# Hymba decoder layer: where the weight's tiles of the input projection begin in SBUF

## The chip, the cores and the metric

The kernel runs on one core of a Trainium2 chip. The metric is the device time of one execution, in microseconds. It is measured over three runs of the kernel before: median 2932.36 us, lowest 2932.19 us, highest 2941.21 us.

## The reference

One layer of a hybrid decoder over 2048 tokens of width 1024, all float32:

```python
h = RMSNorm(x);  z = h @ W_in + b_in        # 1024 -> 3600 columns, in groups of heads
y = concat[ FoX attention | mLSTM | HGRN2 ] # three causal mixers, each fed by its columns of z
x = x + y @ W_out
x = x + W_down( silu(conv3(h W_up)_gate) * conv3(h W_up)_up ),   h = RMSNorm(x)
```

The result must keep float32 accuracy, so each matmul operand is split into a high part (rounded to the type fp32r) and the low remainder. One product then takes three matmuls: high·high, high·low and low·high.

## The kernel before

The time divides into four stages: the input projection with the mLSTM and HGRN2 mixers woven into it (0 to about 940 us), the FoX attention (to about 1420 us), the output projection (to about 1650 us) and the feed-forward part (to the end).

**The input projection.** The 2048 tokens go in two halves, each in two blocks of 512 tokens. For a block, `z_norm` normalises x, transposes it and leaves `hhi` and `hlo`, each `[128, 8, 512]`: eight slices of the 1024 input features on the partitions, 512 tokens along the row. `z_groups` goes through 14 groups of 256 (two of them 264) output columns. `load_split` (L178) loads a group's weight into `wraw`, in two transfers of four feature slices each; ScalarE copies it to `whi` (L188) and GpSimd subtracts to get `wlo` (L189). Both are `[128, 8, width]` and have two buffers, so that the next group's weight is prepared while one is in use.

All the matmuls of the stage's projection are issued by the helper `mm3` (L193 to L198), eight feature slices by three products. There are two kinds of group:

- *Channel groups* (`ct_group`, L256; four of the 14). The weight is the stationary operand, 128 columns at a time, and the input streams past it: 512 tokens per matmul. 768 matmuls in all.
- *Token groups* (`nat_group`, L269; ten of the 14). The input is stationary, 128 tokens at a time, and the weight streams: 256 columns per matmul (3072 matmuls), or 264 in the two groups that carry gate columns as well (768 matmuls).

Every matmul is preceded by a load of its own 128 stationary columns (LDWEIGHTS, the rows PEld); the load for the next matmul runs while the present one streams. A stationary slice of 128 float32 is 512 bytes of a partition's row.

Between the projection's matmuls come the mixers' (`phase_b`, `phase_c`), which `merge` weaves in, and the order of the instructions on each engine is worked out by a planner that simulates the program with a cost model. So a tile that waits for another buffer can move instructions in this stage. Attention and the second feed-forward product have an order written out by hand.

**The other users of the same pattern.** `phase_out` (L1071) calls the same `mm3` at L198 for the output projection, with `yh`/`yl` stationary and `wohi`/`wolo` streaming, 512 columns. `product` in `ffn_up` (L1252) and `mm` in `ffn_down` (L1409) are the same three products, 512 columns each.

**Small tiles.** `z_stats` (L214) collects the second half's sums of squares in a tile `n8s` of its own. `padz` (L1589) is 96 bytes that nothing reads or writes. In `consts` (L1709) the function `cast` (L1713) loads nine constant masks through one scratch tile `craw` of 512 bytes and casts them; the first is used by `phase_c` at L728. The tag `z` has three buffers, through which every group's results leave (L263, L284).

**Where the tiles lie.** A partition's row is one range of bytes, and the pools hand it out in order; the remainders of the first bytes modulo 512, as the kernel before has them:

```
hhi, hlo (both blocks)            64
whi, wlo, first buffer           192      8448 bytes each = 16.5 x 512,
whi, wlo, second buffer          448      so the two buffers differ by 256
yh, yl, wohi, wolo               448      (output projection)
all operands at L1252 and L1409  448      (feed-forward)
```

A row of `whi` for one feature slice is 256 x 4 = 1024 bytes, or 1056 in the two wider groups, in which each slice begins 32 bytes further on.

Of the kernel before, what the change touches and what calls it, by code (L numbers as in the profile page):

```python
# [10 lines left out]
F32 = mybir.dt.float32  # L11
F32R = mybir.dt.float32r
# [9 lines left out]
P = 128  # L22
T = 2048
D = 1024
DT = D // P
# [81 lines left out]
def rms_scale(k, pool, out, ss, n, epsf, tag):  # L107

    for _ in rms_steps(k, pool, out, ss, n, epsf, tag):
        pass  # L110
# [67 lines left out]
def load_split(k, wp, src, tag="w", n=2):  # L178

    nc = k.nc  # L180
    width = src.shape[1]
    hi = k.t(wp, [P, DT, width], F32R, tag=tag + "hi")
    lo = k.t(wp, [P, DT, width], F32R, tag=tag + "lo")
    for q in range(0, DT, n):
        raw = k.t(wp, [P, n, width], tag=tag + "raw")
        nc.sync.dma_start(raw, src[q * P : (q + n) * P, :].rearrange("(dt p) c -> p dt c", p=P))
        h = hi[:, q : q + n, :]
        nc.scalar.activation(h, raw, AF.Copy)  # L188
        nc.gpsimd.tensor_tensor(lo[:, q : q + n, :], raw, h.bitcast(F32), op=ALU.subtract)  # L189
    return hi, lo  # L190
# [23 lines left out]
def z_stats(k, pz, xbufs):  # L214

    nc = k.nc
    ss = k.t(pz, [P, 8], tag="n8s", bufs=1)
    for b in range(2):
        for t in range(4):
            (x,) = z_load(k, 1, b, xbufs, t, 1)  # L220
            i = 4 * b + t
            nc.scalar.activation(x, x, AF.Square, accum_out=ss[:, i : i + 1])
    rstd = k.t(pz, [P, 8], tag="n8r", bufs=1)
    rms_scale(k, pz, rstd, ss, D, 1.0, "h")
    return rstd
# [1301 lines left out]
def _trunk(ctx, tc, a, out):  # L1527
    nc = tc.nc
    k = K(ctx, tc, a, out)

    def pool(stack, name, bufs, **kw):
        if kw.get("space") is not DRAM:
            kw["reuse_waits"] = "tile"
        return stack.enter_context(tc.tile_pool(name=name, bufs=bufs, **kw))
# [30 lines left out]
    with ExitStack() as ms:  # L1565
        cm = pool(ms, "cmix", 1)

        def mconst(name, shape, dt=F32, src=None):
            t = cm.tile(list(shape), dt, tag=name, name=name)
            if src is not None:  # L1570
                nc.sync.dma_start(t, src)
            return t

        bc = ExitStack()
        pb = pool(bc, "bc", 1, side="right")
        psb = pool(bc, "psb", 3, space=PSUM, side="right")
        k.q2 = pb.tile([P, 4, 2, P], F32, tag="q2", name="q2")
        nc.gpsimd.memset(k.q2, 0.0)
        with ExitStack() as zs:
            pz = pool(zs, "z", 2)  # L1580
            wp = pool(zs, "w", 2)
            psw = pool(zs, "psw", 3, space=PSUM)
            k.gmix = pz.tile([P, D], F32, tag="gmix", name="gmix", bufs=1)
            xb, xw = ((pb, "v", 2), (pb, "p4", 2)), ((pz, "x", 2),)
            k.hts = {}
            for _ in z_norm(k, 0, 0, pz, psw, xb):
                pass
            z = z_groups(k, 0, pz, wp, psw, xb)
            pz.tile([P, 24], F32, tag="padz", name="padz", bufs=1)  # L1589
            state(k, mconst)  # L1590
            for _ in range(ZC):
                next(z)
            consts(k, a, cp, mconst, pz, psw, cm)
            mix = mixers(k, pb, psb)
            merge(z, mix, RZ, XAT)
            late = late_consts(k, a, pz, psw)
            next(late)
            rstd = z_stats(k, pz, xw)
            merge(z, mix, RZ, 8)
            next(late)  # L1600
            xs = z_load(k, 1, 0, xw, 0, 2)
            merge(z, mix, RZ, 4)

            norm = z_norm(k, 1, 0, pz, psw, xw, xs, rstd)
            for _ in range(4):
                next(norm)
                merge(z, mix, RZ, 1)
            for _ in norm:
                pass
            for _ in z:  # L1610
                raise AssertionError("steps")
            merge(z_groups(k, 1, pz, wp, psw, xw, rstd), mix, RZ)
            for _ in mix:
                pass
        bc.close()
        wo = ExitStack()
        wor = ExitStack()
        with ExitStack() as at:

            k.pat = {n: pool(at, "at_" + n, 1) for n in ("ga", "oT", "B0", "B1", "A0", "A1", "V1", "o1")}  # L1620
            pa = pool(at, "att", 2)

            k.pat.update((n, pool(at, "at_" + n, 1)) for n in ("o0", "V0"))

            psa = {"m": pool(at, "psm", 3, space=PSUM, side="right")}
            psa.update((n, pool(at, "ps" + n, b, space=PSUM)) for n, b in (("s", 2), ("pv", 2), ("x", 1)))
            k.ga = k.pat["ga"].tile([P, 512], F32, tag="ga", name="ga", bufs=1)
            nc.sync.dma_start(k.ga, a["out_g"][0:1, 0:512].broadcast_to([P, 512]))
            side = {}
            w = w_out_load(  # L1630
                k, pool(wo, "wo", 1, side="right"), pool(wor, "wor", 1, side="right"), side, WO, WOS
            )
            attention(k, pa, psa, side)
# [75 lines left out]
def consts(k, a, cp, mconst, pz, psum, cm):  # L1709

    nc = k.nc

    def cast(dst, src):  # L1713
        raw = cm.tile([P, P], F32, tag="craw", name=k.nm("craw"))[:, 0 : src.shape[1]]
        nc.sync.dma_start(raw, src)
        nc.vector.tensor_copy(dst, raw)

    k.identb = mconst("identb", [P, P], BF16)
    k.mnat = mconst("mnat", [P, P], BF16)
    k.mtr = mconst("mtr", [P, P], BF16)  # L1720
    k.allneg = mconst("allneg", [P, P], BF16)
    k.cmask = mconst("cmask", [P, 7, HD], U8)
    nc.vector.tensor_copy(k.identb, k.ident)
    cast(k.mnat, a["mnat"])
    cast(k.mtr, a["mtr"])
    nc.vector.memset(k.allneg, NEG)
    for i in range(7):
        cast(k.cmask[:, i, :], a["cmask"][:, i * HD : (i + 1) * HD])

    k.sel8 = mconst("sel8", [72, BH])  # L1730
    nc.sync.dma_start(k.sel8[64:72], a["sel8"])
    k.bd = mconst("bd", [16, BH, P], F32R)
    sc = k.t(pz, [8, BH, P], tag="z", bufs=3)
    nc.vector.tensor_copy(sc, k.sel8[64:72].unsqueeze(2).broadcast_to([8, BH, P]))
    nc.sync.dma_start(k.bd[8:16].bitcast(F32), sc)
    k.sel2 = mconst("sel2", [BH, 2, P], F32, a["sel2"])
    k.gbc = mconst("gbc", [P, 512], F32, a["out_g"][0:1, 512:1024].broadcast_to([P, 512]))
    nc.vector.tensor_scalar(out=k.gbc, in0=k.gbc, scalar1=0.5, scalar2=None, op0=ALU.mult)

    b_in = a["b_in"][0]  # L1740
    pk = k.t(pz, [28, P], tag="pg")

    def row(r, src):
        nc.sync.dma_start(pk[r : r + src.shape[0] // P, :], src.rearrange("(c p) -> c p", p=P))

    row(0, b_in[OFF_BQK : OFF_BQK + 512])
    row(4, b_in[OFF_CQ : OFF_CQ + 512])
    for j in range(4):
        row(8 + 4 * j, a["b_conv_w"][0, j])
    row(24, a["lb_logits"][0])  # L1750
    for r, g in ((26, a["a_q_g"]), (27, a["a_k_g"])):
        for i in range(2):
            nc.sync.dma_start(pk[r : r + 1, i * HD : (i + 1) * HD], g)
    k.col = mconst("col", [P, 28])
    ps = k.t(psum, [P, 28], tag="t", bufs=2)
    nc.tensor.transpose(ps, pk, k.ident[0:28, 0:28])
    nc.vector.tensor_copy(k.col, ps)
    k.bcw = k.col[:, 8:24].rearrange("p (j c) -> p j c", c=4)
    k.gq, k.gk = k.col[:, 26:27], k.col[:, 27:28]
    nc.vector.tensor_scalar(out=k.gq, in0=k.gq, scalar1=HD**-0.5, scalar2=None, op0=ALU.mult)  # L1760

    lg = k.col[:, 24:26]
    lm, lr, lb = mconst("lm", [P, 2]), mconst("lr", [P, 2]), mconst("lb", [P, 2])
    nc.vector.tensor_tensor(lm, lg, lg, op=ALU.subtract)
    nc.scalar.activation(lm, lm, AF.Exp)
    nc.vector.reciprocal(lr, lm)  # L1766
    nc.vector.tensor_tensor(lr, lr, lm, op=ALU.mult)
    nc.vector.tensor_tensor(lb, lr, lr, op=ALU.subtract)
    nc.vector.tensor_scalar(out=lb, in0=lb, scalar1=0.0, scalar2=None, op0=ALU.max)
    k.lba, k.lbb, k.lbn = mconst("lba", [P, 2]), mconst("lbb", [P, 2]), mconst("lbn", [P, 2])  # L1770
    nc.vector.tensor_scalar(out=k.lbb, in0=lb, scalar1=-0.5, scalar2=0.5, op0=ALU.mult, op1=ALU.add)
    nc.vector.tensor_scalar(out=k.lbn, in0=k.lbb, scalar1=-1.0, scalar2=None, op0=ALU.mult)
    nc.vector.tensor_tensor(k.lba, lb, k.lbb, op=ALU.add)
# [45 lines left out]
```

## Time and profile before

| | |
|---|---|
| median of three runs | 2932.36 us |
| the profiled execution | 2937.63 us, its span 2935.5 us |
| TensorE (PE) busy | 2817.4 us, 96% of the span |
| weight loads (PEld) busy | 2342.7 us, 80% |
| VectorE (DVE), ScalarE (ACT), GpSimd (POOL) busy | 68%, 44%, 49% |
| mean granted TensorE clock | 0.977 of full speed |

PE is one row of matmuls, and PEld is the weight loads that run beside them. Matmuls are pipelined, and the records of consecutive ones overlap (a duration of 0.39 us, a start every 0.23 us); what a matmul costs is the distance from its start to the next one's start, which this document calls its pitch.

### The profile page before, as it was taken

To read this page: it belongs to the slowest core of one execution; us is meant where nothing else is said; L and a number is where in the kernel's file an instruction comes from. 1 tells how busy PE (TensorE), PEld (TensorE's weight loads), DVE (VectorE), ACT (ScalarE), POOL (GpSimd) and SP (SyncE) were. 2 spreads that over 40 slices of the span, in tenths; PEclk is the share of its full clock that TensorE was granted. 3 is DMA by queue.
4 is the path that set the end of the run, shared out by engine and by line. 5 is a ranking of instruction groups with operands and counts; after the bars stand their busy time and mean duration, and the time that the engine had idled before them with its cause. 6 is when DMAs were issued, how large, how long until landed. Compare 5 with 4: busy or idle time off the path is not lost. (4 is left out here: it accounts for less than half of the span.)

```text
span 2935.5 us, 42833 instructions
## 1 busy us (share of the span) xinstructions
PE 2817.4 (96%) x15181; PEld 2342.7 (80%) x15181; DVE 2005.9 (68%) x3384; ACT 1280.0 (44%) x2167; POOL 1435.1 (49%) x1199
## 2 busy tenths in 40 slices
PE   7999988999988999999899899999999999999999
PEld 7898987889988666666688788888788888888887
DVE  7337687265786787778546577677797577777655
ACT  4213323132322778878424344444454343444443
POOL 2245452334454577766302366666475644444443
PEclk9999997999999999999999999999999999999999
DMA  4424434333334554342257444444777333333666
GB/s 159 127 93 133 150 96 143 94 108 97 111 107 143 107 114 88 81 92 49 72 179 246 148 155 151 154 148 158 268 247 271 114 108 108 108 105 117 232 214 209
DMA packets 346615, 411.07 MB, mean 140 GB/s; under 512 B 47650, under 2 KB 234096, under 8 KB 343232
## 3 DMA queue, kind: packets, MB, share of 16 engines
q1 hardware_dynamic: 292016, 318.45, 37.2%
q10 hardware_dynamic: 51952, 81.45, 7.6%
q0 software_dynamic: 2432, 8.42, 0.8%
q8 instruction: 120, 1.97, 0.3%
q14 instruction: 95, 0.78, 0.1%
HBM read 280.24 MB, written 127.98 MB: 139 GB/s over the span
## 5 line engine op out<-in xcount | busy, mean ns | idle before, releaser
L1221 POOL TENSOR_TENSOR w<-w,w 128x512 fp32r<-128x512 f32 x302 | 404.8, 1353 | 403.3 <-ACT w L1220 339.2
L1409 PE MATMUL ps<-w,w 128*128 128x512 f32 x1848 | 420.9, 389 | 4.0 <-ACT w L1400 2.0
L1409 PEld LDWEIGHTS ps<-w,w 128*128 128x128 f32 x1848 | 346.6, 188 | 77.6 <-ACT w L1400 2.4
L198 PE MATMUL w<-whi,hhi 128*128 128x256 f32 (+1 forms) x1280 | 370.4, 289 | 3.1 <-DVE lr L1766 2.0
L198 PE MATMUL w<-whi,hlo 128*128 128x256 f32 (+1 forms) x1280 | 371.3, 290 | 0.0
L198 PE MATMUL w<-wlo,hhi 128*128 128x256 f32 (+1 forms) x1280 | 370.4, 290 | 0.6 <-POOL wlo L189 0.6
L898 POOL TENSOR_TENSOR pl<-pf,ph 128x512 fp32r<-128x512 f32 (+2 forms) x240 | 287.8, 1212 | 146.6 <-ACT ph L894 133.3
L1402 POOL TENSOR_TENSOR w<-w,w 128x512 fp32r<-128x512 f32 x154 | 216.3, 1412 | 200.9 <-ACT w L1400 155.4
L1220 ACT ACTIVATE w<-w 128x512 fp32r<-128x512 f32 x302 | 180.4, 627 | 258.7 <-POOL w L1221 86.7
L850 DVE TENSOR_REDUCE mx<-m 128x1 f32<-128x512 f32 (+2 forms) x320 | 190.8, 605 | 91.3 <-PE m L845 63.1
L1401 DVE TENSOR_TENSOR w<-w,w 128x512 fp32r<-128x512 f32 x154 | 179.9, 1178 | 103.4 <-ACT w L1399 102.0
L198 PEld LDWEIGHTS w<-whi,hhi 128*128 128x128 f32 x1280 | 245.2, 192 | 4.8 <-issue 3.8
L198 PEld LDWEIGHTS w<-wlo,hhi 128*128 128x128 f32 x1280 | 244.9, 191 | 2.7 <-POOL wlo L189 1.0
L198 PEld LDWEIGHTS w<-whi,hlo 128*128 128x128 f32 x1280 | 244.7, 191 | 1.8 <-issue 0.5
L892 ACT ACTIVATE pf<-s 128x512 f32<-128x512 f32 (+1 forms) x320 | 172.5, 539 | 91.1 <-PE s L886 50.9
L1226 DVE TENSOR_TENSOR w<-w,w 128x512 f32<-128x512 f32 x176 | 149.8, 870 | 85.3 <-DMA w<-in_w_up_dram 81.0
L189 POOL TENSOR_TENSOR wlo<-wraw,whi 128x1024 fp32r<-128x1024 f32 (+1 forms) x56 | 135.3, 2433 | 111.7 <-ACT whi L188 102.2
L894 ACT ACTIVATE ph<-pf 128x512 fp32r<-128x512 f32 (+1 forms) x320 | 185.1, 578 | 10.3
L1267 DVE SCALAR_TENSOR_TENSOR u<-ps,fcol,u 128x1023 f32<-128x1023 f32 x88 | 108.9, 1279 | 95.3 <-ACT u L1266 95.3
L913 PE MATMUL pv<-pl,V 128*65 128x512 f32 (+1 forms) x320 | 121.7, 380 | 25.2 <-DVE pl L898 24.3
L1400 ACT ACTIVATE w<-w 128x512 fp32r<-128x512 f32 x154 | 96.6, 628 | 111.3 <-PE ps L1409 88.7
L1399 ACT ACTIVATE w<-w 128x512 fp32r<-128x512 f32 x154 | 95.9, 623 | 89.8 <-POOL w L1402 44.4
(374 smaller groups left out, 7092.1 us busy)
## 6 DMA issues: line engine op xcount, KB each, us to landing
w<-in_w_up_dram SPq DMA_DIRECT2D x182, 256.0 KB
w<-s_g SPq DMA_DIRECT2D x154, 256.0 KB
w<-in_w_down_dram SPq DMA_DIRECT2D x110, 256.0 KB
wraw<-in_w_in_dram SPq DMA_DIRECT2D x48, 512.0 KB
s_g<-u ACTq DMA_DIRECT2D x88, 256.0 KB
w<-s_w SPq DMA_DIRECT2D x88, 256.0 KB
s_g<-w ACTq DMA_DIRECT2D x66, 256.0 KB
x<-in_x_dram SPq DMA_DIRECT2D x32, 512.0 KB
```

The costliest lines, as they stand in the source:

```text
L189: nc.gpsimd.tensor_tensor(lo[:, q : q + n, :], raw, h.bitcast(F32), op=ALU.subtract)
L198: nc.tensor.matmul(out, lsl(lhs[a], i), rsl(rhs[b], i), start=(i == 0 and j == 0), stop=(i == n - 1 and j == 2))
L850: nc.vector.tensor_reduce(mx[:, i, kb : kb + 1], m[:, 0:n], axis=AX.X, op=ALU.max)
L892: nc.scalar.activation(pf[:, c0:], s[:, c0:], AF.Exp)
L894: nc.scalar.activation(ph[:, c0:], pf[:, c0:], AF.Copy)
L898: eng.tensor_tensor(pl[:, c0:], pf[:, c0:], ph[:, c0:].bitcast(F32), op=ALU.subtract)
L1220: nc.scalar.activation(h, t, AF.Copy)
L1221: nc.gpsimd.tensor_tensor(lo, t, h.bitcast(F32), op=ALU.subtract)
L1226: nc.vector.tensor_tensor(t, x, y, op=op)
L1401: nc.vector.tensor_tensor(gl, gr, gh.bitcast(F32), op=ALU.subtract)
L1402: nc.gpsimd.tensor_tensor(wl, wr, wh.bitcast(F32), op=ALU.subtract)
L1409: nc.tensor.matmul(tiles[tile], g[x][:, tile * P : (tile + 1) * P], w[y], start=j == 0 and c == 0, stop=j == nj - 1 and c == 2,)
```

## The change

The two weight tiles get a fixed size of 17 x 128 float32 (8704 bytes, 17 x 512), of which the group uses the first 8 x width. To make room, and to move the pool's start, three small things go: `n8s` is taken from the existing tag `ss` (two buffers, otherwise used by the query and key groups), `padz` is removed, and `cast` takes its scratch from the tag `z` in place of `craw`.

```diff
@@ load_split
-    hi = k.t(wp, [P, DT, width], F32R, tag=tag + "hi")
-    lo = k.t(wp, [P, DT, width], F32R, tag=tag + "lo")
+
+    hi, lo = (
+        k.t(wp, [P, 17 * P], F32R, tag=tag + x)[:, 0 : DT * width].rearrange("p (n c) -> p n c", c=width)
+        for x in ("hi", "lo")
+    )
@@ z_stats
-    ss = k.t(pz, [P, 8], tag="n8s", bufs=1)
+    ss = k.t(pz, [P, 16], tag="ss")[:, 0:8]
@@ _trunk
             z = z_groups(k, 0, pz, wp, psw, xb)
-            pz.tile([P, 24], F32, tag="padz", name="padz", bufs=1)
             state(k, mconst)
@@ consts, cast
-        raw = cm.tile([P, P], F32, tag="craw", name=k.nm("craw"))[:, 0 : src.shape[1]]
+        raw = k.t(pz, [P, P], tag="z", bufs=3)[:, 0 : src.shape[1]]
         nc.sync.dma_start(raw, src)
         nc.vector.tensor_copy(dst, raw)
```

## Rows read from the trace of the kernel before

**Rows 1.** The page's head: span, busy time, PE in 40 slices and its clock.

```profile
span 2935.5 us, 42833 instructions
PE 2817.4 (96%) x15181; PEld 2342.7 (80%) x15181; DVE 2005.9 (68%) x3384; ACT 1280.0 (44%) x2167; POOL 1435.1 (49%) x1199
PEclk9999997999999999999999999999999999999999
```

**Rows 2.** Busy time by stretch: length, then busy us (instructions) of each engine, clock.

```profile
core 0: us, PE busy (x) PEld busy (x) DVE busy (x) ACT busy (x) POOL busy (x), PEclk, DMA share, GB/s
0.00:480.00 480.00, 440.54 (x3098) 407.82 (x3098) 302.64 (x657) 152.68 (x247) 186.29 (x187) 0.97 0.41 128
480.00:940.00 460.00, 441.31 (x3155) 405.71 (x3154) 294.47 (x646) 125.98 (x200) 188.34 (x180) 0.98 0.34 106
```

**Rows 3.** What TensorE waited for from 13 to 940 us: total, times, longest.

```profile
PE t L395 <- POOL z L391: 7.6, 6, 2.8
PE b L546 <- DVE cstate L763: 3.7, 1, 3.7
PE w L198 <- DVE lr L1766: 2.0, 1, 2.0
...
PE w L198 <- DVE cmask L1716: 1.1, 1, 1.1
```

**Rows 4.** Groups of matmuls by line and form: output<-inputs, count, busy and mean duration.

```profile
L198 PE MATMUL w<-whi,hlo 128*128 128x256 f32 x1024 | 297.9, 291 | 0.0
...
L198 PE MATMUL w<-hhi,wlo 128*128 128x512 f32 x256 | 101.7, 397 | 0.0
...
L198 PE MATMUL w<-whi,hlo 128*128 128x264 f32 x256 | 73.7, 288 | 0.0
```

**Rows 5.** Timeline, a channel group: start, duration, tile; 33 like them lie between.

```profile
111.10 0.39 PE L198 MATMUL w<-hlo,whi 128*128 128x512 f32 x1
...
119.03 0.39 PE L198 MATMUL w<-hhi,wlo 128*128 128x512 f32 x1
```

**Rows 6.** Timeline, output projection: 7 like them between the first two, 23 after.

```profile
1503.50 1.04 PE L1086 MATMUL ty<-ident,yin 128*128 128x128 f32 x8
...
1504.61 0.40 PE L198 MATMUL w<-wolo,yh 128*128 128x512 f32 x1
...
1506.46 0.39 PE L198 MATMUL w<-wohi,yh 128*128 128x512 f32 x1
...
1511.90 0.39 PE L198 MATMUL w<-wohi,yh 128*128 128x512 f32 x1
```

**Rows 7.** Timeline, second feed-forward product, 19 matmuls merged into one row.

```profile
2099.79 4.47 PE L1409 MATMUL ps<-w,w 128*128 128x512 f32 x19
```

**Rows 8.** Timeline, a token group of 256 columns; 94 like them lie between.

```profile
554.72 0.28 PE L198 MATMUL w<-whi,hhi 128*128 128x256 f32 x1
...
565.99 0.28 PE L198 MATMUL w<-whi,hlo 128*128 128x256 f32 x1
```

**Rows 9.** Timeline, a token group of 264 columns (38 between), and the mixer's matmuls after.

```profile
736.20 0.28 PE L198 MATMUL w<-whi,hlo 128*128 128x264 f32 x1
...
740.93 0.28 PE L198 MATMUL w<-whi,hlo 128*128 128x264 f32 x1
741.06 1.05 PE L721 MATMUL b<-q,c 128*128 128x128 f32 x8
```

**Rows 10.** Timeline of DVE: the seven mask casts, first and last.

```profile
25.75 0.20 DVE L1716 CAST cmask<-craw 128x64 uint8<-128x64 f32 x1 [2.48 <-DMA craw<-in_cmask_dram]
...
46.90 0.20 DVE L1716 CAST cmask<-craw 128x64 uint8<-128x64 f32 x1 [0.96 <-DMA craw<-in_cmask_dram]
```

**Rows 11.** Timeline of SP's queue: a weight load, and cast loads that hold the queue.

```profile
32.14 0.93 SPq L186 DMA_DIRECT2D wraw<-in_w_in_dram  x1
...
39.10 6.39 SPq L1715 DMA_DIRECT2D craw<-in_cmask_dram  x2
```

**Rows 12.** The tile of the masks: instruction, count, min/median/max ns, first and last start.

```profile
L728 DVE COPY_PREDICATED att<-cmask,b x56: 635/726/1355, 129.3 to 855.7; 128x512 f32<-128x512 uint8 x40, 96x512 f32<-96x512 uint8 x8, 64x512 f32<-64x512 uint8 x8
```

## The prediction, made before the changed kernel ran

> **What bounds the kernel now.** I read the page's head first: PE is busy for 2817.4 of 2935.5 us, and its clock is at or near full speed in every slice [rows 1]. No other engine is near that. Then the stretches of the input projection: in its two halves PE is busy for 440.54 of 480 us and 441.31 of 460 us, at a mean clock of 0.97 and 0.98, so of 940 us it stands idle for 58; DVE, the next, is busy for 597 [rows 2]. Then PE's waits: they are many and short, none over 3.7 us in what is shown, and mostly for the mixers' operands; a matmul of the projection itself hardly waits [rows 3]. So this stage lasts as long as the matmuls issued in it take, and a matmul costs its pitch. The count per product and form is 1024 of 256 columns, 256 of 264 and 256 of 512, each for three products: 3072, 768 and 768 [rows 4].
>
> The pitch comes out of the timeline. A channel group: 34 pitches in 119.03 - 111.10 = 7.93 us, 233.2 ns for 512 columns [rows 5]. The same helper line in the output projection, same engine, same shape, same order of the three products: 24 pitches in 1511.90 - 1506.46 = 5.44 us, 226.7 ns [rows 6]. The second feed-forward product: 19 matmuls in 4.47 us, less 0.39 for the last one's own duration, 4.08 / 18 = 226.7 ns [rows 7]. What differs between the slow place and the two quick ones and is visible in the program is where the operands begin: at the quick places stationary and streaming tile have the same remainder modulo 512 bytes, in the channel groups they lie 128 bytes apart either way (64 against 192 or 448). Token groups have the same unequal remainders: 95 pitches in 565.99 - 554.72 = 11.27 us, 118.6 ns for 256 columns [rows 8]; and 39 in 740.93 - 736.20 = 4.73 us, 121.3 ns for 264 [rows 9]. No place in the trace shows a settled 256-column stream of this kind with equal remainders.
>
> **What the change does to the remainders.** The removed `craw` (512 bytes, ahead of the input's tiles) moves everything behind it by a whole 512. The removed `n8s` (32 bytes) and `padz` (96) lie between the input's tiles and the weight's: the pool of the weight starts 128 bytes earlier, 192 becomes 64, the input's remainder. The new size, 8704 = 17 x 512, gives the second buffer the same. In the 264-column groups only every slice's own offset stays: 1056 bytes is 32 more than two times 512, so one slice in eight is equal.
>
> **Channel groups.** 768 matmuls go from 233.2 to 226.7 ns: -6.5 x 768 = -5.0 us. Bounds: 0 if the remainder is not the reason; I see no room below 226.7, which both quick places share.
>
> **Token groups, 256 columns.** Not shown by the trace. The ends: a gain as large per matmul as in the channel groups, -6.5 x 3072 = -20.0 us; and a loss. For the loss the nearest row is an unsettled stretch of the output projection: right after other matmuls its first eight pitches, at equal remainders, average 1.85 / 8 = 231.3 ns, 4.6 above its settled value [rows 6]; if token groups never settle at the new place and pay that on top of what they have, +4.6 x 3072 = +14.1 us. Between them I take the share that the nearest row has, the same helper at 512 columns: 226.7 / 233.2 = 0.972, so 115.3 ns and -3.3 x 3072 = -10.1 us.
>
> **Token groups, 264 columns.** One slice in eight changes; at -3.3 ns that is 768 / 8 x 3.3 = 0.3 us. I take 0, with ends of -0.3 and +0.3.
>
> **What is lost again.** In the stage's 940 us PE issues 6253 matmuls [rows 2], of which 4608 are the projection's; the other 1645 come mostly in bundles of eight [rows 9], some 205 interruptions, one for every 22 matmuls of the projection. The first eight after an interruption show 231.3 in place of 226.7 [rows 6], so about a third of the matmuls show a third of the gain. I take a quarter off: -15.1 becomes -11.3 us. Then the idle time: while PE is quicker, the mixers' operands come from DVE, ACT and POOL at the same time as before, and the waits for them [rows 3] get longer. DVE is busy for 597 of 940 us, so most of the time it has slack; I take a tenth off, -10.2 us (none to a third: -11.3 to -7.5).
>
> **The masks' scratch.** In the trace the seven casts of `cmask` stretch from 25.75 to 46.90 us, 3.5 us apart, since each load must wait for the cast before it [rows 10]. The result is first used at 129.3 us [rows 12]. Now nine casts take turns in the three buffers of `z`, after the group results allocated before them and ahead of those after: three rounds of 3.5 us, 10.6 us, in which the groups' results queue for a place. PE is covered by its three PSUM tiles in this pool, each 24 matmuls, 3 x 24 x 0.1213 = 8.7 us; 1.9 us stick out at worst. The queue behind it: these loads are issued by SP in order, and a pair of them has held the queue for 6.39 us [rows 11], with the next group's weight loads behind. If the planner puts a weight load behind such a pair, PE can stand for up to that. Below nothing: the wait for a cast that PE has now, 1.1 us, can go [rows 3]. Range -1.1 to +8.3; I take 0, as the masks are needed 80 us later and the planner is free to spread them. The `ss` place for the second half's sums is one of two, used next by the key groups; no added instruction, so 0, and if a group waits for it, PE has the three PSUM tiles as cover.
>
> A page speaks against the change. The Trainium skill, "SBUF — State Buffer", section "Who interferes with whom", says that TensorE has two independent read ports, one for the streaming operand and one for the weight load, and that it never waits on anyone. By this the begin of a tile could not matter, and the sum would be 0. The trace does not settle it: the two pitches of one line at one shape [rows 5, 6] say that something costs 6.5 ns, not that it is the address.
>
> **Sum.** The profiled execution took 2937.63 us, 2.1 of it outside its span; the median of the three runs is 2932.36, 5.3 lower, and the runs reach from 2932.19 to 2941.21. The gain of 10.2 us comes off the stage in either: 2927.4 from the profiled execution, 2922.2 from the median. I predict 2922.
>
> **Rivals.**
> - *The gain is per matmul, not per column.* Token groups lose the full 6.5 ns: -5.0 - 20.0 = -25.0, a quarter and a tenth off: -16.9 us, 2915.5. For it: what differs per matmul is one weight load, the same in both kinds. Against it: token groups now have a smaller excess to lose. From half of the 512-column pitch at the quick places, 113.4 ns, they are only 5.2 away.
> - *Only the channel groups gain.* In token groups the stream (256 columns) is hardly longer than the weight load beside it, so that the load's own length may set the pitch. Then -5.0, with the same deductions -3.4 us: 2929.
> - *Nothing moves, the remainder is not the reason* (the page's rule above): 2932. For it: equal remainders stand at the quick places together with other differences (absolute place, fewer interruptions). Against it: after an interruption the output projection does return to 226.7 within eight matmuls, and the channel group, over 34 undisturbed ones, does not [rows 5, 6].
> - *Slower.* Equal remainders are bad where load and stream are about equally long: token groups stay in the unsettled regime, +14.1 us, less the channel groups' 5.0 x 0.75 = 3.8: +10.3, 2942.7. It decides from a pitch of 118.6 + (8.8 + 3.8) / 3072 = 122.7 ns upwards. The masks' 8.3 us alone stay below what can be told, but with no gain beside them they come near.
>
> **How the numbers follow.** A measurement of this kernel tells about 0.3%, 8.8 us, from no change: faster is below 2923.6, slower above 2941.2. Forecast: 0.42, and as its own range is 2917 to 2927 (by the two deductions and the masks), some 0.30 of it lies below 2923.6 and 0.12 in between. Per matmul: 0.18, all faster. Channel groups alone: 0.16, same. Nothing: 0.13, of which 0.01 slower through the masks. Slower: 0.11, of which 0.09 above 2941.2. That makes 0.48 faster, 0.42 same, 0.10 slower. The range of 8 in 10 leaves out a part of the slower case and the far end of the per-matmul case: 2910 to 2938.
>
> **What would show it.** Right: the pitch of the channel groups over thirty undisturbed matmuls near 226.7, without its present spread; that of 256-column token groups near 115; 264-column groups unchanged at 121; PE's waits in the first 940 us a few us longer; the start of attention some 10 us earlier, and everything behind it of the same length. Wrong: channel groups still at 233 (the remainder is not the reason); token groups at 118 or above (the case of equal lengths); a wait of PE of several us between 50 and 90 us behind a weight load or a `z` result (the masks). The prediction fails as a whole if the start of attention moves by less than 3 us or by more than 20.

## The result, and the profile after

The changed kernel takes 2947.08 us (median of 9 runs, 2944.88 to 2951.54); the kernel before, run beside it, 2932.36 us (9 runs, 2930.18 to 2941.21). The ratio is 1.0044, 95% interval 1.0032 to 1.0056: slower, by 9 to 16 us. The profiled execution took 2946.67 us, 9.0 more than that of before; the medians lie 14.7 apart, since the profiled execution of before took 5.3 more than its kernel's median. What follows accounts for the 9. The forecast was 2922 us, with a range to 2938.

Line numbers of after are 3 higher in this stage (L198 is L201) and 2 higher in `consts` (L1716 is L1718). The page's head, which answers to [rows 1]: the busy time of PE is the same to the tenth, and the span is 9.2 us longer.

```profile
span 2944.7 us, 42835 instructions
PE 2817.4 (96%) x15181; PEld 2347.0 (80%) x15181; DVE 1996.6 (68%) x3384; ACT 1279.4 (43%) x2167; POOL 1435.2 (49%) x1199
PEclk9999997999999999999999999999999999999999
```

Attention's first matmul, in the timeline of PE, starts at 948.42 us; in the trace of before it was at 939.06. So the input projection's stage has grown by 9.4 us, and all the stages behind it together by nothing. Stretches, as [rows 2], and then the whole stage:

```profile
948.42 0.28 PE L848 MATMUL m<-KB,QB 70*128 70x256 f32 x1
```

```profile
0.00:480.00 480.00, 433.25 (x3067) 405.13 (x3067) 292.84 (x635) 150.39 (x243) 185.66 (x185) 0.96 0.40 125
...
0.00:948.40 948.40, 881.48 (x6245) 817.94 (x6246) 589.25 (x1300) 277.80 (x447) 373.56 (x366) 0.96 0.37 116
```

PE idles for 948.4 - 881.5 = 66.9 us of the stage. The same row of before (0 to 939.1 us) has 880.99 busy, 58.1 idle. So nearly the whole loss is idle time, 8.8 us, and PE's busy time has hardly changed. PE's waits, as [rows 3], name the idle time. The first row is new; the second was 0.3 us before, while others fell (the third from 7.6), and the wait for a mask's cast, 1.1 us before, is gone:

```profile
PE w L201 <- DVE pg L297: 8.9, 1, 8.9
PE w L201 <- ACT hhi L174: 4.7, 2, 3.0
PE t L398 <- POOL z L394: 4.6, 3, 2.5
```

**The new wait.** It is one gap, in the second token block, where the planner weaves the groups `ci` and `bv` into each other. The last 96 matmuls of the two (82 of `bv`, 14 of `ci`) took 14.1 us before (62.7 to 76.7) and take 23.0 now (61.4 to 84.3); the expectations below call them the second `bv` group, this text calls them the piece. Before, PE stood for 2.0 us in the piece (DVE lr L1766 in [rows 3]); now it stands for 8.9, so that 6.9 are new. PE's timeline around the gap:

```profile
70.30 0.28 PE L201 MATMUL w<-whi,hlo 128*128 128x264 f32 x1
79.46 0.56 PE L201 MATMUL w<-whi,hhi 128*128 128x264 f32 x1 [8.88 <-DVE pg L297]
...
80.70 0.42 PE L201 MATMUL w<-whi,hlo 128*128 128x264 f32 x1
80.92 0.42 PE L201 MATMUL w<-whi,hhi 128*128 128x264 f32 x1
...
83.98 0.28 PE L201 MATMUL w<-whi,hlo 128*128 128x264 f32 x1
```

PE has filled its three PSUM tiles and waits until DVE adds the bias and empties one. DVE's timeline shows why it doesn't: between 67.28 and 78.82 us it writes no group's result into a `z` buffer, and the masks' casts stand in that time.

```profile
66.59 0.69 DVE L309 TENSOR_TENSOR z<-w,bias 128x512 f32<-128x512 f32 x1
...
72.59 0.22 DVE L1718 CAST mnat<-z 128x128 bf16<-128x128 f32 x1
...
77.82 0.52 DVE L1718 CAST cmask<-z 128x64 uint8<-128x64 f32 x3 [2.62 <-DMA z<-in_cmask_dram]
...
78.82 0.42 DVE L292 TENSOR_TENSOR z<-w,bias 128x256 f32<-128x256 f32 x1
79.16 0.16 DVE L297 TENSOR_TENSOR pg<-w,bias 128x8 f32<-128x8 f32 x1
```

The loads behind these casts, in SP's queue; the three in one row hold the queue while they wait for a buffer:

```profile
67.73 0.47 SPq L1717 DMA_DIRECT2D z<-in_mnat_dram  x1
...
69.62 4.02 SPq L1717 DMA_DIRECT2D z<-in_cmask_dram  x3
...
78.04 0.33 SPq L1717 DMA_DIRECT2D z<-in_cmask_dram  x1
```

The gap costs a second time. The clock was granted at 1.00 before it, is at 0.50 (1.2 GHz) in it, and is back at 1.00 in the stretch from 85 us: a 264-column matmul has a pitch of 0.22 us meanwhile (80.70 to 80.92) in place of 0.12. The 20 pitches from 79.46 to 83.98 take 4.5 us in place of 2.4. So the piece's loss of 8.9 us is 6.9 of waiting and some 2 of clock.

```profile
77.00:79.00 2.00, 0.00 (x0) 0.00 (x0) 1.12 (x5) 0.00 (x0) 0.00 (x0) 0.50 0.99 291
...
81.00:83.00 2.00, 2.00 (x11) 2.00 (x11) 0.56 (x3) 0.00 (x0) 0.00 (x0) 0.50 0.20 66
83.00:85.00 2.00, 2.00 (x14) 1.96 (x14) 0.34 (x1) 0.29 (x1) 0.00 (x0) 0.77 0.03 8
85.00:87.00 2.00, 2.00 (x10) 1.65 (x9) 0.16 (x2) 1.72 (x2) 1.15 (x1) 1.00 0.40 133
```

**The pitches.** A channel group (answers to [rows 5]), then the same token group as in [rows 8], then a group of 264 columns ([rows 9]); first and last matmul of an unbroken stretch:

```profile
106.70 0.39 PE L201 MATMUL w<-hhi,whi 128*128 128x512 f32 x1
...
117.36 0.39 PE L201 MATMUL w<-hhi,wlo 128*128 128x512 f32 x1
...
563.51 0.28 PE L201 MATMUL w<-whi,hhi 128*128 128x256 f32 x1
...
574.90 0.28 PE L201 MATMUL w<-whi,hlo 128*128 128x256 f32 x1
...
744.83 0.28 PE L201 MATMUL w<-whi,hlo 128*128 128x264 f32 x1
...
749.54 0.28 PE L201 MATMUL w<-whi,hlo 128*128 128x264 f32 x1
```

47 pitches in 10.66 us make 226.8 ns; 95 in 11.39 make 119.9; 39 in 4.71 make 120.8. The mean pitch in ns over all the groups, from the starts of consecutive matmuls and without those that follow an interruption (anything above 1.2 times the median); the last column is the difference times the number:

```
                 before    after    number   us
512 columns      232.6     227.7      768   -3.8
256 columns      118.6     119.6     3072   +3.1
264 columns      121.1     121.2      768   +0.1
```

So the begin of a tile does act on the pitch, in opposite directions in the two kinds of group, and the sum is nearly nothing.

### The profile page after: what moved, and what is told of

The parts are those of the page before. It is cut to its first block, busy times and chain, and to the rows that moved or that the text cites. A ratio compares the mean times of both kernels' runs of the same rounds, so it can differ in the third digit from the quotient of the medians.

```text
span 2944.7 us, 42835 instructions
## 1 busy us (share of the span) xinstructions
PE 2817.4 (96%) x15181; PEld 2347.0 (80%) x15181; DVE 1996.6 (68%) x3384; ACT 1279.4 (43%) x2167; POOL 1435.2 (49%) x1199
## 5 line engine op out<-in xcount | busy, mean ns | idle before, releaser
L201 PE MATMUL w<-whi,hhi 128*128 128x256 f32 (+1 forms) x1280 | 372.6, 291 | 8.9 <-DVE pg L297 8.9
L201 PE MATMUL w<-whi,hlo 128*128 128x256 f32 (+1 forms) x1280 | 373.6, 292 | 0.0
L201 PE MATMUL w<-wlo,hhi 128*128 128x256 f32 (+1 forms) x1280 | 372.7, 291 | 0.6 <-POOL wlo L192 0.6
L201 PEld LDWEIGHTS w<-whi,hhi 128*128 128x128 f32 x1280 | 248.9, 194 | 10.3 <-issue 9.2
L201 PEld LDWEIGHTS w<-wlo,hhi 128*128 128x128 f32 x1280 | 248.8, 194 | 2.7 <-POOL wlo L192 1.0
L201 PEld LDWEIGHTS w<-whi,hlo 128*128 128x128 f32 x1280 | 248.5, 194 | 1.8 <-issue 0.5
L1229 DVE TENSOR_TENSOR w<-w,w 128x512 f32<-128x512 f32 x176 | 151.4, 879 | 84.3 <-DMA w<-in_w_up_dram 79.8
L897 ACT ACTIVATE ph<-pf 128x512 fp32r<-128x512 f32 (+1 forms) x320 | 185.1, 578 | 10.3
```

The lines of the kernel that those rows point to most:

```text
L201: nc.tensor.matmul(out, lsl(lhs[a], i), rsl(rhs[b], i), start=(i == 0 and j == 0), stop=(i == n - 1 and j == 2))
L897: nc.scalar.activation(ph[:, c0:], pf[:, c0:], AF.Copy)
L1229: nc.vector.tensor_tensor(t, x, y, op=op)
```

## The experiments

All numbers of a kernel's stage are from its one profiled execution; "attention" is the start of attention's first matmul. Two executions of one kernel start it 1.2 and 1.6 us apart (e10 and e11 below), so that differences of this size say nothing. Each ratio is to the kernel before as run beside that experiment, where its median was 2939.6 to 2941.0 us; the times are not to be compared with the 2932.36 above. The diffs are cut to the lines that matter.

**Whose are the 9 us: e1 to e3, and e7.** The first takes the masks' scratch out of `z` and keeps the rest of the change:

```diff
-        raw = k.t(pz, [P, P], tag="z", bufs=3)[:, 0 : src.shape[1]]
+        raw = k.t(pb, [P, P], tag="c", bufs=3)[:, 0 : src.shape[1]]
```

> The changed kernel, with the masks' scratch taken from the mixers' tag c (three buffers, first used by the mixers at about 118 us) in place of the tag z; the remainders stay equal. Theory (the masks' nine casts in the z buffers hold up the second bv group): TensorE's wait of 8.9 us on DVE line 297 goes, that group takes about 14 us again in place of 23.0, attention starts at 938 to 941 us in place of 948.4, and the time is within 4 us of the kernel before. Rival (the new place of the weight, by its pitch or by another plan, is what costs): the wait goes, but attention still starts 5 us or more later than in the kernel before, and the time stays at +8 us or more.

Measured: 2940.54 us, ratio to before 0.9996 (0.9982 to 1.0010); attention at 937.5; the piece takes 14.4 us; pitches as in after (227.7, 119.6). The casts now run long before the piece, at a time when the mixers don't use their tag yet, and the wait in the piece is as long as the 2.0 us of before:

```profile
18.61 0.22 DVE L1718 CAST mnat<-c 128x128 bf16<-128x128 f32 x1
...
28.19 1.80 DVE L1718 CAST cmask<-c 128x64 uint8<-128x64 f32 x3 [2.69 <-DMA c<-in_cmask_dram]
```

```profile
PE w L201 <- DVE pg L297: 2.0, 1, 2.0
```

The second does the reverse, the kernel before with only its masks' scratch in `z` (`cm.tile(... "craw")` becomes the first line of the diff above):

> The kernel before with only the masks' scratch moved to the tag z; weight tiles, padding and sums as before, remainders 192 and 448 against 64. Theory (masks): the second bv group grows by about 9 us, attention starts 7 to 11 us later, the time is +8 to +14 us; pitches stay at 232 to 233 ns for 512 columns and 118.6 ns for 256. Rival (the weight's place): no more than 3 us change.

Measured: 2953.2 us, ratio 1.0051 (1.0036 to 1.0066); attention at 948.9; the piece 22.9 us; pitches as before the change (232.4, 118.6). PE's timeline has the same gap:

```profile
80.45 0.56 PE L198 MATMUL w<-whi,hhi 128*128 128x264 f32 x1 [8.96 <-DVE pg L294]
```

The third changes the dose: the seven parts of `cmask` in one load and one cast, three tiles of `z` in place of nine.

```diff
-        raw = k.t(pz, [P, P], tag="z", bufs=3)[:, 0 : src.shape[1]]
+        raw = k.t(pz, [P, BLK], tag="z", bufs=3)[:, 0 : src.shape[1]]
-    for i in range(7):
-        cast(k.cmask[:, i, :], a["cmask"][:, i * HD : (i + 1) * HD])
+    cast(k.cmask.rearrange("p i d -> p (i d)"), a["cmask"])
```

> The changed kernel with the masks loaded in three pieces instead of nine (all seven level masks in one transfer and one cast), still through the tag z. Theory (the rounds of casts through three buffers set the wait): one round in place of three, so TensorE's wait at the second bv group falls from 8.9 us to 0 to 4 us, and attention starts 5 us or more earlier than in the changed kernel. Rival (not the number of casts but that these tiles stand in line at all, behind the results of the group before): the wait stays above 6 us.

Measured: 2943.17 us, ratio 1.0005 (0.9993 to 1.0018); attention at 937.2; the piece 16.9 us; the wait is there still, and shorter:

```profile
74.12 0.56 PE L201 MATMUL w<-whi,hhi 128*128 128x264 f32 x1 [3.49 <-DVE pg L297]
```

The loss goes with the masks' tiles in `z`: it comes with them alone (e2), goes without them (e1), and shrinks with their number (e3, where the wait is 1.5 us above that of e1). The sums' tile was run by itself, in the existing tag `ss`, with the pad enlarged by the 32 bytes that this frees:

```diff
-    ss = k.t(pz, [P, 8], tag="n8s", bufs=1)
+    ss = k.t(pz, [P, 16], tag="ss")[:, 0:8]
-            pz.tile([P, 24], F32, tag="padz", name="padz", bufs=1)
+            pz.tile([P, 32], F32, tag="padz", name="padz", bufs=1)
```

> The kernel before with only the small sums moved to a double-buffered tile of their own and the pad enlarged, so that no large tile moves. Theory: no difference, attention starting at 939 within 1 us, ratio 0.999 to 1.001. Rival (the sums' new tile moves other small tiles or lets a norm start earlier): attention 2 us or more away from 939.

Measured: 2940.14 us, ratio 0.9993 (0.9980 to 1.0006), attention at 938.9. It costs nothing.

**What in the masks' edit holds TensorE: e8 and e9.** In the trace of after three things coincide: casts in DVE's queue ahead of the adds, loads that hold SP's queue, and nine tiles that pass through `z`'s three buffers ahead of `bv`'s results.

```diff
e8   -        nc.vector.tensor_copy(dst, raw)
e8   +        nc.gpsimd.tensor_copy(dst, raw)
e9   -        nc.sync.dma_start(raw, src)
e9   +        nc.scalar.dma_start(raw, src)
```

> The changed kernel with the nine casts of the masks issued on POOL instead of DVE; the scratch stays in tag z. In the changed kernel TensorE waits 8.9 us in the second bv group for two adds of DVE that stand behind casts which wait for their loads. Theory A (the rotation of the three z buffers holds the group's result: its place comes free only when the masks ahead of it have been loaded and cast): the wait stays, second bv group 21 to 24 us, attention start 946 to 950, ratio about 1.004. Theory B (DVE's queue is what holds the adds: they need nothing of the masks, but stand behind casts in order): the wait goes, second bv group 14 to 16 us, attention start 937 to 940, ratio about 0.999.

> The changed kernel with the nine loads of the masks issued on ACT's queue instead of SP's; scratch in tag z, casts on DVE. Theory A (the rotation of z): no great change, second bv group 20 to 24 us, attention start 945 to 950. Theory C (what costs is the hold of SP's queue: three mask loads take 4.0 us in it, and a weight load stands behind them): second bv group 14 to 17 us, attention start 937 to 940.

Measured: e8 2952.44 us, ratio 1.0039 (1.0027 to 1.0051), attention at 951.7, the piece 23.5 us; e9 2949.1 us, 1.0030 (1.0014 to 1.0046), attention at 950.8, 23.3 us. Both attention starts lie beyond what theory A expected, by 1.7 and 0.8 us. PE's longest wait in e8, then in e9 (us in total, times, longest):

```profile
PE w L201 <- DVE pg L297: 9.8, 1, 9.8
```

```profile
PE w L201 <- DVE pg L297: 9.6, 1, 9.6
```

In e8 DVE has no cast of the masks in its queue, and does its add only when POOL has cast enough of them. Between the nine masks and `bv`'s result one more tile goes through `z` (L1736), so with three buffers the result takes the place of the eighth mask, whose cast on POOL ends at 80.42 + 0.30 = 80.72; the add starts at 80.75:

```profile
80.42 0.30 POOL L1718 CAST cmask<-z 128x64 uint8<-128x64 f32 x1 [0.24 <-DMA z<-in_cmask_dram]
```

```profile
80.20 0.41 DVE L1736 COPY z<-sel 8x512 f32<-8x512 f32 x1 [5.01 <-POOL cmask L1718]
80.75 0.43 DVE L292 TENSOR_TENSOR z<-w,bias 128x256 f32<-128x256 f32 x1
```

Neither queue by itself is the cause (both moved at once wasn't tried). What e1, e2, e3, e8 and e9 have in common is theory A: the wait is 8.9 to 9.8 us whenever the nine tiles pass through `z`'s three buffers, 3.5 with three tiles, and with none 2.0, as before the change.

**What the begin of a tile does: e4 to e6.** On e1, every group's weight begins at a distance of its own inside the tile (`o` floats), so that one execution shows many distances (the table of `o` for each group is left out here):

```diff
-def load_split(k, wp, src, tag="w", n=2):
+def load_split(k, wp, src, tag="w", n=2, o=0):
-        k.t(wp, [P, 17 * P], F32R, tag=tag + x)[:, 0 : DT * width]
+        k.t(wp, [P, 17 * P], F32R, tag=tag + x)[:, o : o + DT * width]
```

> As the kernel with the masks' scratch in tag c, but each group's weight begins at its own distance from the tile's start: for the 256-column token groups 0, 16, 32, 48, 64, 96, 128, 160, 192, 224, 256, 320, 384, 448, 480 and 512 bytes, for the channel groups 0, 16, 32, 64, 128, 192, 256 and 384 bytes, so that one trace gives the pitch for each distance from the input's remainder. Theory (the distance modulo 512 sets the pitch, in opposite senses for the two kinds): channel groups at 226.7 ns for 0 and about 233 ns for 128 and 384; token groups at 120.0 ns for 0 and 512 and 118.6 ns for 128 and 384; other distances in between or beyond. Rival (equal or unequal is all that counts, or the absolute place): one value for 0 and one other value for every other distance.

Measured: attention at 937.1, one run of 2943.0 us. The mean pitch in ns (without those above 1.15 times the group's median) by the distance of the weight's begin from the input's remainder, in bytes; before the change it was 128 or 384:

```
512 columns   0: 227.7   16: 229.8   32: 233.2   64: 233.3  128: 232.7  192: 229.6  256: 227.2  384: 232.4
256 columns   0: 119.7   16: 118.0   32: 117.0   48: 118.4   64: 117.8   96: 119.8  128: 119.3  160: 117.4
            192: 116.9  224: 118.3  256: 119.8  320: 117.6  384: 118.6  448: 116.5  480: 118.2  512: 119.6
```

Where two distances differ by 256, the pitches agree within 0.7 ns (0 and 256, 64 and 320, 128 and 384, 192 and 448, 224 and 480; 0 and 512). A distance of 0 (or 256) is best for 512 columns, and among the worst for 256. So the expected period of 512 bytes fails here already. These are different groups with different neighbours, so two distances were put to all eight 256-column groups at once, `o` = 48 floats (e5) and 112 (e6), with 0 for the rest:

> The changed kernel with the masks' scratch taken from the mixers' pool (as in e1_masks_c), and with the 256-column token groups' weight tiles begun 192 bytes after the input's remainder; the channel groups keep the equal remainder. Theory (the distance between the two operands' addresses, with a period of 256 bytes, sets the pitch of these matmuls, and each kind has its own best distance): 256-column matmuls at about 117 ns instead of 119.6, so 3072 x 2.6 = 8 us less than e1_masks_c, attention starting near 929.5 instead of 937.5, and a ratio to the kernel before near 0.997. Rival (the spread among the groups of the scan came from what the groups share the queues and engines with, not from the address): pitch 119 to 120 in most groups, attention near 937, ratio 0.999 to 1.000.

> As e5_nat192, with 448 bytes, 256 more. Theory with a period of 256 bytes: the same pitch (116.5 to 117.5) and the same time as e5_nat192. Rival (period of 512 bytes, as the change's wording has it): the two differ, by as much as the 192 and 448 of the scan and more, 1 ns or over per matmul, 3 us in all.

Measured: e5 2935.55 us (12 runs; before 2940.1), ratio 0.9980 (0.9968 to 0.9991); e6 2936.47 us, 0.9984 (0.9972 to 0.9996). The pitch of 256 columns is 115.9 and 116.1: lower than expected, and the same at 192 and 448, so the period is 256 bytes, not the 512 of the change's wording. In all these runs the weight alone was moved and the input stayed at its remainder of 64. For 512 columns it is the distance that counts, not the weight's own place: with the weight at 448 a channel group shows 232.4 (e4, distance 384), and the output projection, with both operands at 448, 226.7 [rows 6]. For 256 columns no run tells the two apart. Within a group it settles at either of two values. A stretch of e5 at the lower one, 32 pitches in 3.63 us, 113.4 ns, half of the 512-column pitch:

```profile
837.75 0.28 PE L201 MATMUL w<-whi,hlo 128*128 128x256 f32 x1
...
841.38 0.28 PE L201 MATMUL w<-wlo,hhi 128*128 128x256 f32 x1
```

By these intervals e5 and e6 are quicker than the kernel before, by 0.1 to 0.3% and by 0.04 to 0.28%. But less came of it than the pitch gave: 3072 x (119.6 - 115.9) = 11.4 us against e1, while attention in e5 starts at 933.9, only 3.6 us earlier.

**Where the other 8 us went.** The idle time of the stage is nearly that of e1 (59.2 and 60.3 us). The clock differs. In stretches of 2 us from 13 us to attention, busy time times what is missing to full clock sums to 28.9 us in e5 and 20.8 in e1 (before 24.6, after 28.4): 8.1 more, and 3.6 + 8.1 is 11.7. One place of it: in e5 PE stands for 2.25 us for `b_cols`, and the clock then is 0.50; in e1 it stands for 1.73 us there, and the clock stays at 1.00. The rows of e5, then the stretch of e1 around its own wait:

```profile
843.91 1.46 PE L724 MATMUL b<-q,c 128*64 128x128 f32 x8 [2.25 <-DVE b_cols L533]
```

```profile
844.00:846.00 2.00, 2.00 (x11) 1.67 (x12) 1.69 (x7) 0.56 (x2) 0.00 (x0) 0.60 1.07 371
846.00:848.00 2.00, 2.00 (x7) 1.16 (x7) 1.90 (x9) 1.09 (x2) 0.22 (x1) 0.50 0.50 157
848.00:850.00 2.00, 2.00 (x11) 2.00 (x11) 1.96 (x3) 1.11 (x2) 2.00 (x2) 0.50 0.00 0
```

```profile
846.00:848.00 2.00, 1.36 (x11) 1.22 (x12) 1.86 (x8) 0.63 (x1) 0.21 (x1) 1.00 1.02 342
848.00:850.00 2.00, 2.00 (x15) 1.58 (x14) 1.90 (x9) 1.24 (x2) 0.00 (x0) 1.00 0.87 282
```

Whether these falls belong to the program was tried by a second profiled execution of each of the two kernels:

> The kernel of e5_nat192 profiled a second time. In e5_nat192 the time that the clock took from TensorE before attention (busy time times what is missing to full clock, over stretches of 2 us from 13 us on) was 28.8 us, in e1_masks_c 20.9, and attention started 3.6 us earlier in place of the 11.4 that the pitches give. Theory (the clock falls where this kernel's own waits are, so it belongs to the program): 27 to 30 us again, the stretch 844 to 850 us at 0.5 again, attention within 1 us of 933.9. Rival (the falls differ from execution to execution): a loss that is 3 us or more off, and an attention start that is off by as much.

> The kernel of e1_masks_c profiled a second time. Theory as for e10_nat192_look2: a clock loss of 20 to 22 us, attention within 1 us of 937.5. Rival: a loss that is 3 us or more off.

Measured: e10, 29.9 us lost to the clock and attention at 935.2 (1.2 from the first, just outside what was expected); e11, 25.4 us lost and attention at 939.1, so the second expectation failed. At the wait for `b_cols` the clock falls to 0.50 again in e10 (2.23 us of waiting), and it falls there in e11 too (1.80 us), where it had stayed up in e1. The pitches repeat within 0.2 ns, the falls only in part. Over two executions each, e5's kernel loses 29.4 us and e1's 23.1, 6.3 more, and starts attention at 934.5 and 938.3. With a spread of 4.6 us between two executions of one kernel that is little evidence; all the runs say the same, roughly. The mean granted clock of e5's 12 executions is 0.9766, 0.0021 below the kernel before beside it; e1's 12 are 0.0002 below theirs. The difference of 0.0019 of 2933 us makes some 6 us (an estimate). And the ratios, 0.9980 and 0.9996, lie 4.7 us apart, not 11.4. That the quicker stream pays about half of its gain to the clock is likely from this; which waits make the clock fall, and how much of it another plan would avoid, stays open.

## Why the prediction was wrong

**What bounds the kernel, and the method.** This held: the change acts inside the input projection's stage alone, and the stages behind kept their length. The stage itself was forecast 10.2 us shorter and came out 9.4 longer. By the terms below the pitches gave -0.6 us in place of -15.1, and the masks' piece +8.9 in place of 0; the remaining 1 us is the sum of smaller waits and of the clock.

**Channel groups, -5.0 us.** Right in mechanism, a little too large: the pitch went to 227.7, not 226.7, from a mean of 232.6, not the 233.2 of the one group read: -3.8 us. That the begin of the operands is the reason, which the prediction took from two places that differed in more than that, is shown by the runs: e2 keeps the old begins and the old pitch, e1 has the new ones and 227.7, and e4 spreads the same four groups from 227.2 to 233.3 by the begin alone.

**Token groups of 256 columns, -10.1 us.** This step failed. It took over the share by which 512 columns gain (0.972) and expected 115.3 ns; measured, 119.6, +3.1 us. The sign is the other one: at 256 columns equal remainders are near the worst distance (e4). Two things differ from a channel group, the width and the roles (in a token group the input is stationary and the weight streams). No run separates them in this stage, but the output projection has a token group's roles at 512 columns and equal remainders, and shows 226.7, the good value [rows 6]; that speaks for the width. Why the width should do it, no run shows. The bound above nothing was on record (+14.1 us), but its reason was not what happened: the pitch is settled (the middle half of all in after, by size, is at 120 ns; before it reached from 117 to 121), only at a worse value. The value hoped for does exist, at 192 bytes, where e5 shows 115.9.

**Token groups of 264 columns.** 0, as predicted.

**The deductions** (a quarter and a tenth) had no gain to work on. e5 shows what they would have been worth: of 11.4 us, 3.6 arrived in the first pair of profiled executions and 3.8 in the mean of two, so some two thirds were lost, not a third, and likely the greater part to the clock, which the prediction left out.

**The masks' scratch, 0 (range -1.1 to +8.3).** This step failed, and it made the result. The length of the rotation was nearly right: from the issue of the first load to that of the last, 67.73 to 78.04 = 10.3 us (10.6 predicted). That is partly luck, since it was not three equal rounds: the first cast came only at 72.59, behind other work of DVE. What was wrong is the cover. The prediction set three whole PSUM tiles against the rotation, 8.7 us. But the first load was issued at 67.73, when two of the three tiles were full and PE had just begun on the third (the last 24 matmuls before the gap start at 67.5): it went on to 70.30 + 0.28 = 70.58, and 2.85 us of cover were left, one tile. From 67.73 to PE's next matmul at 79.46 are 11.73 us, and 11.73 - 2.85 = 8.88, the wait. "The planner is free to spread them" did not come true: in the traces of after, e8 and e9 the first eight masks all go through `z` ahead of `bv`'s next result. SP's hold of the queue, the second mechanism named, is not what costs (e9). The high end of +8.3 was near in size (8.9, of which 6.9 are new), but that was luck: 6.4 of it stood for SP's hold. The low end, -1.1 for the wait for a cast, came true beside it. The prediction said that with no gain beside it this time would come near to what can be told, and gave the combination 0.01. That a gap also costs clock, some 2 us here, was no term of the sum.

**The small sums, 0.** Right (e7).

**The rivals.** None of them is what happened. The slower one had the right side and nearly the right time (2942.7). Its condition, that equal remainders are bad in token groups, came true with 1.0 ns in place of 4.6, 3.1 us of 14.1; the rest of the loss is the masks'. So its time is luck. "Nothing moves" is refuted: moving the begin alone moves the pitch by up to 6 ns. The Trainium skill, "SBUF — State Buffer", section "Who interferes with whom", says that PE never waits on anyone and that its two read ports are independent. These traces disagree so far as TensorE's own two operands go: the 512-column pitch is 227.2 or 233.3 ns, and the 256-column one 115.9 or 119.6, by where the weight's tile begins. Which port, bank or bus makes it so, no run here shows.

**What the prediction would have recognised.** Both of its signs of failure were there: token groups at 118 ns or above, and a wait of PE of several us between 50 and 90 us behind a `z` result.

## What to carry to other kernels

A scratch tile put into a rotating tag (a set of buffers handed out in turn) can hold up whoever allocates next there for its whole time in the rotation; count the cover that the consumer has left when the rotation starts, not all the buffers that it has. A gain per matmul that was measured at one width and one role of the operands need not carry over to another: try a few begins in one run, each group with its own, before the layout is rebuilt for one of them. A second change made only to free the space deserves its own line in the sum, and its own run.

## What was not expected of the hardware

- The pitch of the three-product stream depends on where the weight's tile begins, measured from the input's, modulo 256 bytes: 227.2 to 233.3 ns at 512 columns, 116.5 to 119.8 at 256 columns (e4), and the distance that is best at 512 columns is among the worst at 256.
- At the good distance (192 bytes, e5) 256 columns settle at 113 or at 118 ns from one stretch to the next, in one kernel; 113.4 is half of 226.7.
- After an idle stretch of 8.9 us TensorE ran at 0.50 of its clock for another 4 to 5 us. Idle stretches of about 2 us inside the woven mixers did the same in some executions and not in others (843 to 852 us: in e5, e10 and e11, not in e1).
